# The start of a hybrid decoder step: weights by contraction tiles in a written order, and one unit of the decode's logits moved behind the projections

## The chip, the cores and the metric

The kernel runs on one core of one Trainium2 chip. A core has five engines that run side by side and wait for one another through semaphores: TensorE (PE, matrix products and transposes, with its own stream of weight loads, PEld), VectorE (DVE), ScalarE (ACT), GpSimd (POOL) and SyncE (SP), which here only issues transfers. SP, POOL and ACT put transfers on queues that sixteen DMA engines serve. Products are accumulated in PSUM, in banks of 512 float32 columns. The metric is the device time of one execution in microseconds; before the change it is 1644.03 us, the median of three runs (1642.79 to 1644.74).

## The reference

One layer of a decoder step for 512 prompt rows, 16 learned meta rows ahead of them and 8 x 4 sample rows that continue sequences with 512 cached positions. All 560 rows are normalized and multiplied by one combined weight of 2048 x 12288; what comes out is used by a stick-breaking attention and a gated short convolution; both are merged, projected and normalized once more. Everything is float32.

```python
h = rmsnorm(x, g_pre)
q, k, v, ga, cb, cc, ch, gc, ma, mc = split(h @ w_in)
a = stick_breaking(q, k, v) * silu(ga)            # prompt: its own rows; samples: cached pages, then own rows
c = cb * causal_conv3(cc * ch) * silu(gc)
m = sigmoid(ma + b_ga) * (a @ w_pa) + sigmoid(mc + b_gc) * (c @ w_pc)
y = x + rmsnorm(m @ w_out, g_post)

# stick_breaking for one head
z = q @ k.T * d ** -0.5 + b_sb                     # logits
log_keep = where(s < t, log_sigmoid(-z), 0)
after = reverse_cumsum(log_keep) - log_keep
out = where(s < t, exp(log_sigmoid(z) + after), 0) @ v
```

## The kernel before

Rows of activations lie transposed: `h_hi` and `h_lo` hold the normalized rows as 16 contraction tiles of 128 by 560 rows. A float32 product is made of three products of a reduced type: each operand is split in a high part (a cast on ACT) and the rest (a subtraction on DVE), and a product is high by high, high by low, low by high. So each weight tile of 128 x 1024 costs a load on SP's queue, a cast `whi` on ACT, a subtraction `wlo` on DVE and 24 products for each range of rows. Five raw buffers (`wraw`) and three pairs of split buffers (`whl`) go round.

**The start** (lines 143 to 363) normalizes the 560 rows in five tiles, 0 to 4, and makes the first four query heads (`FIRST`). `norm_stats` loads a tile, squares and sums its rows on ACT and takes Ln and Exp for a first reciprocal root, which `newton` mends with five small operations of one column on DVE. `norm_half` multiplies half a tile by that root and the gain (DVE), transposes eight blocks on PE into two PSUM tiles, copies them as high parts (ACT), and returns the function that later subtracts the low parts (DVE). The PSUM tiles for the transposes come round from three banks `z` and one `t`. The gain is spread over the partitions by 32 small products and four copies on DVE (`g_copy`). `q_load` brings the weights of one query head in two tiles, one for each half of the contraction, in rows of 128 columns; `q_part` multiplies all 16 contraction tiles for one head. The rows come in two ranges (`START`), the first of 256 rows, which the token tiles 0 and 1 fill. What is wrapped in `pin` (`keep_in_program_order`) keeps the written order on its engine; the rest is ordered by a planner that simulates a timeline and prefers earlier program order, or whatever stands in `high_priority`. Here DVE's work is pinned, while loads, ACT's work and PE's products and transposes are left to the planner, the transposes with high priority.

**Projections** (824 to 833): for heads 0 to 3 `head_now` makes keys, values and another query head and attends at once; for heads 4 to 7 `head_later` makes keys and values only. **Pairs** (1016 to 1042): 4 pairs of the attention's gate, 16 of the convolution, 16 of the merge gates, each two columns of weights by seven products instead of eight (`seven`, line 887). **w_pc stage** (1079 to 1095): the convolution's output by `w_pc`, the last four heads' attention, and the decode's values. Then `w_pa`, merge, `w_out` and the output norm.

**The decode** (`decode_steps`, a generator) is spread over these stages. Its logits are 16 units of four pages each, a page being one step: two products and sums over 128 x 1024 elements on DVE and ACT (lines 689 to 700), with loads on POOL's queue. `DEC1` units belong to the part `"part"`, which the projections call up: five steps in each `head_now`, four in each `head_later`, until the part is used up. The others belong to `"logits"` and are called up by `dec_group` behind each of the 36 pair groups: groups 1 to 4 take 2, 1, 2, 1 steps, groups 5 to 20 one each, 21 to 31 two and one in turn from two on, group 32 all that is left. Then come two softplus pieces, the weights (two exponentials) and the values: 64 pages of 256 KB through seven buffers `vpage`, multiplied on PE at line 784. The first value pages have to be asked for by the end of the pairs (line 1043).

Of the kernel before, what the change touches and what calls it, by code (L numbers as in the profile page):

```python
# [9 lines left out]
F32 = mybir.dt.float32  # L10
# [7 lines left out]
P = 128  # L18
# [29 lines left out]
DEC1 = 6  # L48
# [12 lines left out]
def hybrid_step_kernel(  # L61
# [64 lines left out]
    def rstd_of(eng, out, ss, tmp, n, w=1, later=False):  # L126

        v, r, t = (tmp[:n, i * w:(i + 1) * w] for i in range(3))
        act.activation(r, ss, AF.Ln, bias=eps_c[:n], scale=1.0 / D)
        act.activation(r, r, AF.Exp, scale=-0.5)  # L130
# [54 lines left out]
    def norm_stats(i):  # L185

        n = sum(r[0] for r in XT[i][0])
        xt = sp.tile([P, D], F32, name="xt", bufs=3)[:n]
        load_x(xt, i)
        ss = sp.tile([P, 1], F32, name="ss", bufs=5)[:n]  # L190
# [3 lines left out]
        with tc.high_priority():  # L194
            act.activation(sq, xt, AF.Square, accum_out=ss)
            newton = rstd_of(dve, rs, ss, tmp, n, later=True)
        return (i, n, xt, rs), newton

    def norm_half(c, x):
# [7 lines left out]
        low = []  # L207
        for kq in range(2):
            pt = next(start_ps)()
            pv = pt[:, :4 * n].rearrange("p (k t) -> p k t", t=n)  # L210
            with tc.high_priority(2000):
                for k in range(4):
                    pe.transpose(out=pv[:, k, :], in_=hn[:, (4 * kq + k) * P:(4 * kq + k + 1) * P],
                                 identity=ident[:n, :n])
            k0 = 8 * c + 4 * kq
            for r0, r1, t0 in XT[i][1]:
                dst = (slice(None), slice(k0, k0 + 4), slice(t0, t0 + r1 - r0))
                with tc.high_priority(2000):
                    act.copy(h_hi[dst], pv[:, :, r0:r1])
                low.append((h_lo[dst], pv[:, :, r0:r1], h_hi.bitcast(F32)[dst]))  # L220

        def lows():
            for x in low:
                pin(dve.tensor_sub(*x))
        return lows


    def w_load(src, pl=wraw):
        raw = pl.tile([P, 8, P], F32, tag="raw", name="raw", bufs=5 if pl is wraw else 2 * FIRST - 5)
# [53 lines left out]
    w_low = []  # L283

    def low(n=1):

        for _ in range(n):
            unit, raw = w_low.pop(0)
            lo = whl.tile([P, 8, P], F32R, tag="lo", name="wlo")
# [1032 lines left out]
```

## Time and profile before

| what | us |
|---|---|
| median of three runs (lowest, highest) | 1644.03 (1642.79, 1644.74) |
| the profiled execution's own time | 1641.85 |
| its span, first to last instruction | 1640.3 |
| busy in the span: PE / DVE / ACT / POOL | 1594.9 / 1251.8 / 970.1 / 232.4 |
| start, until the first product of the projections | 86.4 |
| projections | 86 to 386 |
| pairs | 386 to about 1176 |
| w_pc stage | about 1176 to 1342 |

The times in the timeline rows are microseconds from the span's first instruction: start, length, engine, line, operation, what is written and read, its size. In brackets stands how long the engine had been idle and what ended that. Lengths of products overlap, since the next starts while one drains; what a product costs is the distance to the next start. An engine's name with a q (SPq) is its issuing of transfers.

### The profile page before, as it was taken

What the parts mean: (1) busy time and instruction counts of PE and PEld (TensorE: products, weight loads), DVE (VectorE), ACT (ScalarE), POOL (GpSimd) and SP (SyncE); (2) the same over time, 40 slices, a digit from 0 to 9 for tenths busy, and PEclk for the clock granted to TensorE, in tenths of its full rate; (3) what the DMA queues carried; (4) which work ended last, traced back from release to release, by engine and by line L of the source; (5) the groups of instructions that cost most, each with busy time, mean ns of one, the idle gap of its engine ahead of it and who ended that gap; (6) DMA issues with size and microseconds to landing.
All of it is one profiled execution on the core that took longest, in us unless ns stands there. A gap on an engine that the chain in (4) does not pass through costs nothing.

```text
span 1640.3 us, 31584 instructions
## 1 busy us (share of the span) xinstructions
PE 1594.9 (97%) x12176; PEld 1531.3 (93%) x12176; DVE 1251.8 (76%) x1707; ACT 970.1 (59%) x2529; POOL 232.4 (14%) x414
## 2 busy tenths in 40 slices
PE   7999999999999999999999999999999999999996
PEld 6999999999999999999999999989867699999995
DVE  4537887797988988888988888876555567877774
ACT  5237887745765655655677667685544543455552
POOL 0033233322101010101011010013122110000000
PEclk7999999999999999999999999999999999999998
DMA  9255454445544444443455454446887555433336
GB/s 228 70 179 152 155 160 139 146 128 170 157 147 136 136 135 122 127 142 111 137 164 161 149 174 148 135 125 204 283 261 222 172 152 179 154 106 94 104 87 216
DMA packets 306492, 252.72 MB, mean 154 GB/s; under 512 B 11457, under 2 KB 276741, under 8 KB 305237
## 3 DMA queue, kind: packets, MB, share of 16 engines
q1 hardware_dynamic: 277605, 159.73, 34.1%
q0 software_dynamic: 28016, 88.80, 16.5%
q8 instruction: 95, 1.56, 0.4%
q10 hardware_dynamic: 720, 2.17, 0.4%
q14 instruction: 56, 0.46, 0.1%
HBM read 217.95 MB, written 32.71 MB: 153 GB/s over the span
## 4 chain that ended last, share of the span: by engine, by line
PE 75%; ACT 6%; DMA 5%; DVE 5%; issue 3%; POOL 0%; DVEq 0%; SPq 0%; POOLq 0%; ACTq 0%
PE mm L887 24%; PE mm L252 24%; PE o L887 19%; ACT junk L695 3%; PE tp L784 2%; ACT whi L236 2%; DMA raw<-in_w_in 2%; PE z L614 1%; PE o L624 1%; DVE pr L689 1%; DVE wlo L237 1%; DMA gt<-gate_scr 1%; PE z L545 1%; PE z L887 1%; DMA kpage<-in_cache_k 1%
## 5 line engine op out<-in xcount | busy, mean ns | idle before, releaser
L236 ACT CAST whi<-raw 128x1024 fp32r<-128x1024 f32 x251 | 263.1, 1050 | 258.5 <-PE o L887 79.3
L237 DVE TENSOR_TENSOR wlo<-raw,whi 128x1024 fp32r<-128x1024 f32 x251 | 306.4, 1221 | 58.0 <-ACT whi L236 46.1
L887 PE MATMUL mm<-h_hi,whi 128*128 128x272 f32 (+1 forms) x1152 | 333.5, 290 | 2.8 <-ACT whi L236 2.8
L887 PE MATMUL mm<-h_lo,whi 128*128 128x272 f32 (+1 forms) x1152 | 332.1, 288 | 0.0
L887 PE MATMUL mm<-h_hi,wlo 128*128 128x272 f32 (+1 forms) x1152 | 331.3, 290 | 0.0
L887 PE MATMUL o<-t_hi,whi 128*128 128x272 f32 (+1 forms) x864 | 252.2, 292 | 8.5 <-ACT o L901 5.9
L887 PE MATMUL o<-t_hi,wlo 128*128 128x272 f32 (+1 forms) x864 | 249.9, 289 | 1.4 <-DVE wlo L237 1.4
L887 PE MATMUL o<-t_lo,whi 128*128 128x272 f32 (+1 forms) x864 | 249.6, 289 | 0.0
L237 DVE TENSOR_TENSOR wlo<-s,whi 128x1024 fp32r<-128x1024 f32 x126 | 154.2, 1224 | 101.5 <-ACT whi L236 101.2
L887 PEld LDWEIGHTS mm<-h_hi,whi 128*128 128x128 f32 x1152 | 217.3, 189 | 5.5 <-ACT whi L236 3.7
L887 PEld LDWEIGHTS mm<-h_hi,wlo 128*128 128x128 f32 x1152 | 216.3, 189 | 0.6 <-DVE dr L412 0.4
L887 PEld LDWEIGHTS mm<-h_lo,whi 128*128 128x128 f32 x1152 | 216.8, 188 | 0.1
L695 ACT ACTIVATE junk<-pr 128x128 f32<-128x128 f32 x592 | 182.7, 309 | 28.3 <-DVE pr L689 16.1
L236 ACT CAST whi<-s 128x1024 fp32r<-128x1024 f32 x126 | 131.6, 1044 | 97.5 <-PE o L887 31.0
L252 PE MATMUL mm<-h_hi,whi 128*128 128x280 f32 (+1 forms) x640 | 187.1, 293 | 0.0
L252 PE MATMUL mm<-h_hi,wlo 128*128 128x280 f32 (+1 forms) x640 | 187.0, 293 | 0.0
L252 PE MATMUL mm<-h_lo,whi 128*128 128x280 f32 (+1 forms) x640 | 186.7, 292 | 0.0
L887 PEld LDWEIGHTS o<-t_hi,whi 128*128 128x128 f32 x864 | 162.7, 188 | 15.1 <-ACT o L901 7.0
L887 PEld LDWEIGHTS o<-t_hi,wlo 128*128 128x128 f32 x864 | 162.9, 189 | 2.3 <-DVE wlo L237 2.2
L887 PEld LDWEIGHTS o<-t_lo,whi 128*128 128x128 f32 x864 | 163.4, 189 | 0.0
L689 DVE TENSOR_TENSOR pr<-kpage,qb 128x1024 f32<-128x1024 f32 x128 | 152.3, 1218 | 8.4 <-DMA kpage<-in_cache_k 4.0
L252 PEld LDWEIGHTS mm<-h_hi,whi 128*128 128x128 f32 x640 | 120.5, 188 | 0.7
(389 smaller groups left out, 3398.2 us busy)
## 6 DMA issues: line engine op xcount, KB each, us to landing
raw<-in_w_in SPq DMA_DIRECT2D x192, 512.0 KB, 4.3
kpage<-in_cache_k POOLq DMA_DIRECT2D x64, 256.0 KB, 3.4
qb<-q_scr POOLq DMA_DIRECT2D x32, 512.0 KB, 5.3
vpage<-in_cache_v POOLq DMA_DIRECT2D x64, 256.0 KB, 5.7
raw<-in_w_out SPq DMA_DIRECT2D x32, 512.0 KB, 4.0
gate_scr<-g POOLq DMA_DIRECT2D x32, 272.0 KB, 3.2
gt<-gate_scr POOLq DMA_DIRECT2D x16, 544.0 KB, 4.2
raw<-in_w_pc SPq DMA_DIRECT2D x16, 512.0 KB, 5.8
```

What stands on the lines that cost most here:

```text
L236: act.copy(hi, x)
L237: dve.tensor_sub(lo, x, hi.bitcast(F32))
L252: pe.matmul(o, lhsT=w, rhs=r[:, t0:t1], start=(k == 0 and n == 0), stop=(k == nk - 1 and n == 2))
L545: pe.matmul(zt[:m, c0:c0 + n], lhsT=l[:, s0:s0 + m], rhs=r[:, ts:ts + n], start=(c0 == 0 and i == 0), stop=(i == 2), skip_group_check=True)
L614: pe.matmul(o, lhsT=l, rhs=x, start=False, stop=(i == len(ops) - 1), skip_group_check=True)
L624: pe.matmul(ot[:, ts - NMETA:ts - NMETA + n], lhsT=l[:m, st, :], rhs=x[:m, c0:c0 + n], start=False, stop=(g == GROUPS[-1] and i == 2), ski ...
L689: dve.tensor_mul(pr, kt.unsqueeze(1).broadcast_to([P, 2, 512]), qt))
L695: act.activation(junk, pr[:, t, h * P:(h + 1) * P], AF.Copy, accum_out=z_all[:, pg, b, 4 * hf + h, 2 * i + t:2 * i + t + 1])
L784: pe.matmul(po[32 * j:32 * (j + 1), :], lhsT=lhs, rhs=rhs, start=(pg == 0), stop=(pg == NPG), tile_position=(0, 32 * j), skip_group_check= ...
L887: pe.matmul(o, lhsT=l[:, k, :], rhs=r, start=(start and k == 0 and m == 0), stop=(stop and k == 7 and m == 2), skip_group_check=True)
```

## The change

The start is written out as one order for every engine: loads of token tiles, statistics, transposes, high parts and products are pinned too. The query weights come as eight tiles of two contraction tiles by four heads, in rows of 512 columns; `q_chunk` multiplies two contraction tiles for all four heads as soon as these are there, over the first range of rows. Two of the gain's copies go to ACT, the Newton operations of tiles 2 and 4 to POOL, the bank `o` joins the transposes' round, and the four accumulators of the first range share two banks. Tile 2 comes before tile 4, and tile 3 last. `DEC1` becomes 5, and the groups take 2 steps each up to the fourth, one each up to 20, two and one in turn up to 33, where the logits end.

```diff
-DEC1 = 6
+DEC1 = 5
...
-            nc.sync.dma_start(xt[r:r + n, :], {"p": xp, "m": meta_tokens, "s": xs}[src][r0:r0 + n, :])
+            tc.keep_in_program_order(
+                nc.sync.dma_start(xt[r:r + n, :], {"p": xp, "m": meta_tokens, "s": xs}[src][r0:r0 + n, :]))
...
     def g_copy(c):
-        pin(dve.tensor_copy(g_bc[:, c * 512:(c + 1) * 512], g_ps[c]))
+        copy = dve.tensor_copy if c < 2 else act.copy
+        pin(copy(g_bc[:, c * 512:(c + 1) * 512], g_ps[c]))
-    start_ps = cycle((z_ps, z_ps, z_ps, t_ps))
+    start_ps = cycle((z_ps, z_ps, z_ps, t_ps, o_ps))
...
-        with tc.high_priority():
-            act.activation(sq, xt, AF.Square, accum_out=ss)
-            newton = rstd_of(dve, rs, ss, tmp, n, later=True)
-        return (i, n, xt, rs), newton
+        pin(act.activation(sq, xt, AF.Square, accum_out=ss))
+        return (i, n, xt, rs), rstd_of(eng, rs, ss, tmp, n, later=True, fix=pin)
...
-            with tc.high_priority(2000):
-                for k in range(4):
-                    pe.transpose(out=pv[:, k, :], in_=hn[:, (4 * kq + k) * P:(4 * kq + k + 1) * P],
-                                 identity=ident[:n, :n])
+            for k in range(4):
+                pin(pe.transpose(out=pv[:, k, :], in_=hn[:, (4 * kq + k) * P:(4 * kq + k + 1) * P],
+                                 identity=ident[:n, :n]))
...
+        def highs():
+            for dst, src in parts:
+                pin(act.copy(h_hi[dst], src))
...
+    def by_k(tile_):
+        return tile_.rearrange("p (k h) c -> p k h c", k=2)
+    def q_load():
+        c = len(q_raw)
+        raw = wraw.tile([P, 8, P], F32, tag="raw", name="raw")
+        pin(nc.sync.dma_start(raw.rearrange("p (k h) c -> p k (h c)", k=2),
+                              win[2 * c * P:2 * (c + 1) * P, GATE_Q:GATE_Q + FIRST * P].rearrange(
+                                  "(k p) c -> p k c", p=P)))
+        q_raw.append(raw)
+    def q_part_tile(c, name):
+        if c < 3:
+            return whl.tile([P, 8, P], F32R, tag=name, name="w" + name)
+        return sp.tile([P, 8, P], F32R, name="w" + name, bufs=NC - 3)
+    def q_high():
+        c = len(q_hi)
+        q_hi.append(q_part_tile(c, "hi"))
+        pin(act.copy(q_hi[c], q_raw[c]))
+    def q_low():
+        c = len(q_lo)
+        q_lo.append(q_part_tile(c, "lo"))
+        pin(dve.tensor_sub(q_lo[c], q_raw[c], q_hi[c].bitcast(F32)))
+    def q_product(o, h, k, n, start, stop):
+        t0, t1 = START[n]
+        hi, lo = (by_k(x[k // 2])[:, k % 2, h, :] for x in (q_hi, q_lo))
+        for m, (l, r) in enumerate(((hi, h_hi), (hi, h_lo), (lo, h_hi))):
+            pin(pe.matmul(o, lhsT=l, rhs=r[:, k, t0:t1], start=(start and m == 0), stop=(stop and m == 2),
+                          skip_group_check=True))
+    def q_chunk(c):
+        for h in range(FIRST):
+            for k in (2 * c, 2 * c + 1):
+                q_product(q_o[h], h, k, 0, k == 0 and h % 2 == 0, k == KD - 1)
+    def keep_warm(n):
+        pass
...
+    X[0], X[1] = x_load(0), x_load(1)
+    for _ in range(3):
+        q_load()
+    X[2] = x_load(2)
+    X[0], newton0 = norm_stats(X[0])
+    g_copy(0), g_copy(1)
+    g_copy(2), g_copy(3)
+    X[1], newton1 = norm_stats(X[1])
+    newton0(pin)
+    h00, l00 = norm_half(0, X[0])
+    h01, l01 = norm_half(1, X[0])
+    h00()
+    newton1(pin)
+    q_high()
+    h10, l10 = norm_half(0, X[1])
+    h01()
+    l00()
+    h11, l11 = norm_half(1, X[1])
+    h10()
+    X[4] = x_load(4)
+    for _ in range(2):
+        q_load()
...
+    l10()
+    q_high()
+    q_low()
+    h11()
+    q_chunk(0)
+    l01()
+    q_low()
+    l11()
+    q_high()
+    q_chunk(1)
+    X[2], newton2 = norm_stats(X[2], pool)
+    q_low()
+    for _ in range(2):
+        q_load()
+    q_chunk(2)
+    X[4], newton4 = norm_stats(X[4], pool)
+    newton2()
+    h20, l20 = norm_half(0, X[2])
+    q_high()
+    q_low()
+    q_load()
+    X[3] = x_load(3)
+    h20()
+    q_chunk(3)
+    h21, l21 = norm_half(1, X[2])
+    q_high()
+    l20()
+    q_low()
+    h21()
+    newton4()
+    q_chunk(4)
+    h40, l40 = norm_half(0, X[4])
+    l21()
+    q_high()
+    h40()
+    q_low()
+    h41, l41 = norm_half(1, X[4])
+    q_chunk(5)
+    l40()
+    h41()
+    q_high()
+    q_low()
+    l41()
+    q_chunk(6)
+    q_high()
+    q_low()
+    X[3], newton3 = norm_stats(X[3])
+    q_chunk(7)
+    newton3(pin)
+    h30, l30 = norm_half(0, X[3])
+    h30()
+    h31, l31 = norm_half(1, X[3])
+    h31()
+    l30()
+    l31()
...
+    for h in range(FIRST):
         q_o[h] = (z_ps if h < 3 else mm_ps)()[:, :START[1][1] - START[1][0]]
-        q_part(q_o[h], q_w[h], 1, (0, 1, 2), True, True)
-        low(min(len(w_low), 2))
+        for k in range(KD):
+            q_product(q_o[h], h, k, 1, k == 0, k == KD - 1)
...
-        if n <= 31:
-            dec_step(1 if 4 < n <= 20 else 1 + n % 2, "logits")
-        elif n == 32:
-            dec_step(64, "logits")
-            dec_step(1)
+        if n <= 33:
+            dec_step(1 if 4 < n <= 20 else 2 if n <= 4 else 1 + n % 2, "logits")
+            if n == 33:
+                dec_step(64, "logits")
         else:
             dec_step(1)
```

More of the change, by code (lines that the diff above doesn't have):

```diff
@@ L189, in norm_stats @@
         load_x(xt, i)
+        return i, n, xt
+    def norm_stats(x, eng=dve):
+        i, n, xt = x
         ss = sp.tile([P, 1], F32, name="ss", bufs=5)[:n]
@@ L206, in norm_half @@
                                      op0=ALU.mult, op1=ALU.mult))
-        low = []
+        parts = []
         for kq in range(2):
@@ L210, in norm_half, with w_load @@
             pv = pt[:, :4 * n].rearrange("p (k t) -> p k t", t=n)
-            with tc.high_priority(2000):
-                for k in range(4):
-                    pe.transpose(out=pv[:, k, :], in_=hn[:, (4 * kq + k) * P:(4 * kq + k + 1) * P],
-                                 identity=ident[:n, :n])
+            for k in range(4):
+                pin(pe.transpose(out=pv[:, k, :], in_=hn[:, (4 * kq + k) * P:(4 * kq + k + 1) * P],
+                                 identity=ident[:n, :n]))
             k0 = 8 * c + 4 * kq
             for r0, r1, t0 in XT[i][1]:
[L217 to L220, printed above, removed]
+                parts.append(((slice(None), slice(k0, k0 + 4), slice(t0, t0 + r1 - r0)), pv[:, :, r0:r1]))
+        def highs():
+            for dst, src in parts:
+                pin(act.copy(h_hi[dst], src))
         def lows():
[L223 to L229, printed above, removed]
+            for dst, src in parts:
+                pin(dve.tensor_sub(h_lo[dst], src, h_hi.bitcast(F32)[dst]))
+        return highs, lows
+    def w_load(src):
+        raw = wraw.tile([P, 8, P], F32, tag="raw", name="raw")
         nc.sync.dma_start(raw, src.rearrange("(k p) c -> p k c", p=P))
@@ L282, in hybrid_step_kernel @@
     START = ((HM, HM + 256), (HM + 256, T))
[L283 to L289, printed above, removed]
-            pin(dve.tensor_sub(lo, raw, unit[0].bitcast(F32)))
-            unit.append(lo)
-    def q_part(o, ws, n, parts, start, stop):
-        t0, t1 = START[n]
-        for k in range(KD):
-            for m in parts:
-                pe.matmul(o, lhsT=ws[k // 8][m // 2][:, k % 8, :], rhs=(h_lo if m == 1 else h_hi)[:, k, t0:t1], start=(start and k + m == 0),
-                          stop=(stop and k == KD - 1 and m == parts[-1]), skip_group_check=True)
@@ L300, in hybrid_step_kernel @@
-    q_w, q_o = [], []
-    def q_load(h):
-        q_w.append([])
-        for src in win_srcs(GATE_Q + h * P):
-            n = len(w_low)
-            raw = w_load(src, sp if n >= 5 else wraw)
-            hi = sp.tile([P, 8, P], F32R, name="whi", bufs=2 * FIRST - 3) if n >= 3 else \
-                whl.tile([P, 8, P], F32R, tag="hi", name="whi")
-            act.copy(hi, raw)
-            q_w[h].append([hi])
-            w_low.append((q_w[h][-1], raw))
-    x0, newton0 = norm_stats(0)
-    x1, newton1 = norm_stats(1)
@@ L345, in hybrid_step_kernel @@
-    l21 = norm_half(1, x2)
-    l20()
-    newton3(pin)
-    l30 = norm_half(0, x3)
-    l21()
-    l31 = norm_half(1, x3)
-    l30()
-    low()
-    l31()
-    low()
-    for h in range(FIRST):
-        q_part(q_o[h], q_w[h], 0, (2,), False, True)
+    q_high()
[9 more added lines that the diff above has]
+    q_high()
```

41 lines of the change are left out of this document (14 added, 27 removed).

## The prediction

> **What bounds the kernel now.** I read the page's busy table first, then the busy time in windows, stage by stage. The columns of a window row are: length, then busy time and instructions of TensorE, its weight loads, VectorE (DVE), ScalarE (ACT) and, where it ran, GpSimd (POOL), then granted clock, DMA share, GB/s.
>
> ```profile
> span 1640.3 us, 31584 instructions
> PE 1594.9 (97%) x12176; PEld 1531.3 (93%) x12176; DVE 1251.8 (76%) x1707; ACT 970.1 (59%) x2529; POOL 232.4 (14%) x414
> ...
> 0.00:26.39 26.39, 14.47 (x67) 11.76 (x67) 12.66 (x31) 15.64 (x24) 2.15 (x9) 0.67 1.02 245
> 26.39:53.44 27.05, 24.32 (x192) 23.35 (x192) 17.71 (x41) 13.63 (x29) 0.00 (x0) 0.94 0.45 107
> 53.44:86.40 32.96, 32.96 (x249) 32.96 (x249) 12.99 (x13) 5.72 (x9) 2.21 (x4) 1.00 0.35 100
> ...
> 86.00:386.00 300.00, 298.87 (x2296) 291.39 (x2294) 231.53 (x322) 208.53 (x672) 94.07 (x164) 1.00 0.48 148
> 490.00:833.00 343.00, 341.64 (x2697) 340.48 (x2696) 305.29 (x369) 205.49 (x545) 27.41 (x48) 1.00 0.44 130
> 833.00:1054.00 221.00, 216.29 (x1698) 214.22 (x1698) 185.47 (x179) 153.85 (x448) 23.95 (x42) 1.00 0.52 155
> 1160.00:1360.00 200.00, 198.88 (x1319) 157.95 (x1318) 121.45 (x261) 97.72 (x164) 35.28 (x65) 1.00 0.68 216
> ```
>
> TensorE is the bound from 53 us to the end of these windows. Of the first 26.39 us it is busy 14.5, at a granted clock of 0.67. So time saved in the start moves everything behind it forward one for one; time taken from DVE or ACT in a stage where TensorE has no gap is worth nothing, and time put there costs only the gaps it opens. The timeline of TensorE shows what the start is made of:
>
> ```profile
> 8.62 1.33 PE L175 MATMUL z<-g_hl,pick 16*128 16x128 f32 x8
> ...
> 13.78 0.42 PE L213 MATMUL z<-ident,hn 128*128 128x128 f32 x1
> 13.99 0.42 PE L213 MATMUL tp<-ident,hn 128*128 128x128 f32 x1
> ...
> 22.07 1.97 PE L213 MATMUL z<-ident,hn 128*128 128x128 f32 x8 [6.80 <-DVE h_lo L224]
> 26.39 1.01 PE L297 MATMUL mm<-h_hi,whi 128*128 128x256 f32 x3 [2.35 <-ACT h_hi L219]
> ...
> 38.97 0.28 PE L297 MATMUL mm<-h_lo,whi 128*128 128x256 f32 x1
> ...
> 42.18 0.28 PE L297 MATMUL o<-h_hi,whi 128*128 128x256 f32 x1
> 44.93 1.06 PE L213 MATMUL z<-ident,hn 128*128 128x128 f32 x8 [2.48 <-DVE hn L205]
> ...
> 47.02 0.27 PE L213 MATMUL tp<-ident,hn 128*128 128x128 f32 x1
> 47.13 0.27 PE L213 MATMUL z<-ident,hn 128*128 128x128 f32 x1
> ...
> 83.81 0.30 PE L297 MATMUL mm<-h_hi,wlo 128*128 128x296 f32 x1
> ...
> 86.27 0.30 PE L297 MATMUL mm<-h_hi,wlo 128*128 128x296 f32 x1
> 86.40 0.29 PE L252 MATMUL mm<-h_hi,whi 128*128 128x280 f32 x1
> ```
>
> From one start to the next, a product with 256 columns takes 0.119 us (27 intervals from 38.97 to 42.18), one with 296 takes 0.137 (18 from 83.81 to 86.27), a transpose 0.21 on the slow clock and 0.11 on the full one. The four first query heads are 192 products of each width: 22.8 + 26.2 = 49.0 us. They start at 26.39 and the next projection starts at 86.40, so 11.0 us of those 60 are transposes, slow clock (the middle window: 27.05 us at 0.94, so 3.2 us at half rate, 1.6 lost) and waits.
>
> **The change, the start.** Products, transposes, normalizations and splits stay the same in number. The weights now come as eight tiles of two contraction tiles by four heads, so the first products need only an eighth of the weights and the first half of two token tiles. The order is written out, so I walked it down, each engine in order, with these durations (ACT, then DVE):
>
> ```profile
> 10.28 1.91 ACT L195 ACTIVATE sq<-xt 128x2048 f32<-128x2048 f32 x1 [1.71 <-DMA xt<-in_x_prompt]
> ...
> 31.12 0.58 ACT L219 CAST h_hi<-z 128x512 fp32r<-128x512 f32 x1
> 31.60 0.59 ACT L219 CAST h_hi<-tp 128x512 fp32r<-128x512 f32 x1
> 36.68 1.92 ACT L195 ACTIVATE sq<-xt 128x2048 f32<-128x2048 f32 x1 [4.49 <-DMA xt<-in_x_prompt]
> ...
> 39.16 1.90 ACT L195 ACTIVATE sq<-xt 128x2048 f32<-128x2048 f32 x1
> ...
> 47.75 0.14 DVE L133 TENSOR_SCALAR rtmp<-ss 128x1 f32<-128x1 f32 x1
> ...
> 48.58 1.28 DVE L205 SCALAR_TENSOR_TENSOR hn<-xt,rs,g_bc 128x1024 f32<-128x1024 f32 x1
> 49.78 0.68 DVE L224 TENSOR_TENSOR h_lo<-z,h_hi 128x512 fp32r<-128x512 f32 x1
> 50.38 0.68 DVE L224 TENSOR_TENSOR h_lo<-tp,h_hi 128x512 fp32r<-128x512 f32 x1
> ...
> 56.23 2.35 DVE L290 TENSOR_TENSOR wlo<-raw,whi 128x1024 fp32r<-128x1024 f32 x2
> ```
>
> So a tile's statistics occupy ACT for 2.5 us (36.68 to 39.16), a copy of 512 columns 0.48; the five Newton operations take DVE 0.83, a normalized half 1.2, a low part 0.6, a weight's low part 1.15. A weight's cast on ACT I take at 0.95, twice the copy of half its width.
>
> ACT: the second tile lands at 10.28. The two gain copies that move from DVE to ACT end by 10.5 (the last gain product starts 8.62 and runs 1.33), so they cost the chain 0.2. Statistics end 13.0, two copies 14.0, first weight cast 14.9, next copies 15.9, and those of the second tile 17.9, behind their transposes. DVE: Newton 13.1 to 13.9, half 15.2, low parts 16.4, half 17.6, low parts 18.8, first weight's low part 19.9, and the next low part at 20.6 frees the PSUM bank that the last four transposes of the second tile want (three banks go round). Those run to 21.6, and behind them in TensorE's queue stands the first chunk of 24 products. It starts at 21.6 instead of 26.39. The clock is slow then: 3.2 us at half rate as now, so the chunk ends at 25.7, the next two at 28.6 and 31.4.
>
> From there a chunk takes 24 x 0.119 = 2.85 us and half a tile's eight transposes 0.88; for the fifth tile, of 48 tokens, I estimate half of that. Chunk 3 ends 35.1, chunk 4 38.8. The fifth tile's second normalized half is written ahead of chunk 5 and comes from DVE at 40.3, so TensorE waits 1.0; it waits 0.5 more for a low part before chunk 6. Chunk 7 ends at 50.0, the last tile's transposes at 51.8, its first low parts at 52.7, and 26.2 us of wide products end at 79.0. With 0.1 us more at each handover the same walk ends at 79.4, with 0.15 at 80.1. I take 79.6: a **gain of 6.8 us** against 86.40, bounds 6.1 (ending at 80.3) and 7.5. Afterwards the next projection can't be late: the three weight slots that it needs are the first chunks', last read by head 3 at 73 to 75, and cast plus low part take 2.2.
>
> Loads: the first 26.39 us move 245 GB/s. A tile of 128x2048 is 1.05 MB, a weight 0.52. The walk wants the third token tile (4.7 MB into the queue) by 23.3 and the fourth weight (5.6 MB) by 28.3; 4.7 MB take 19.2 us at that rate, 5.6 take 22.9. On SP's queue the fifth tile waits for the first one's buffer, free at 12, with two weights behind it; the sixth weight waits for the first low part at 20, and the last tile stands behind the eighth weight, issued at 25 and wanted at 44. Weight rows grow from 512 B to 2 KB, which I count as nothing.
>
> Two Newton chains move to GpSimd, whose own arithmetic this trace shows only in other shapes:
>
> ```profile
> 0.43 0.10 POOL L1310 MEMSET const-float32-0.0<- 128x1 f32 x1 [0.43 <-issue]
> ...
> 1127.08 0.94 POOL L716 TENSOR_SCALAR_AFFINE_SELECT z_new<-z_new 32x256 f32<-32x256 f32 x1
> ```
>
> Between 0.10 and 0.94 an operation I take 0.35, nearer to the memset, which has the same single column. The chain then runs 25.9 to 27.7, the half it feeds ends at 29.0, and TensorE wants it at 31.4: up to 0.85 us an operation is free, and at 1.0 the walk ends at 80.3. [...]
>
> **The change, the decode.** The loop over heads asks for 20 page steps in the first four heads and 16 in the last four; 6 units of 4 pages are 24 steps, 5 are 20. So the four steps of head 4 leave a stage where TensorE waits 1.1 us in 300: gain 0. They go to the second and fourth group of pairs, which get two steps instead of one, and to groups 32 and 33; the softplus, weights and value loads behind them come a group or two later.
>
> ```profile
> 425.00:446.00 21.00, 21.00 (x169) 21.00 (x168) 18.23 (x20) 13.47 (x37) 2.37 (x4) 1.00 0.47 143
> 446.00:468.00 22.00, 22.00 (x177) 22.00 (x177) 19.98 (x22) 17.07 (x57) 2.90 (x5) 1.00 0.60 189
> ...
> 1121.92 4.08 POOL L667 DMA_DIRECT2D vpage<-in_cache_v  x7
> ...
> 1160.00:1200.00 40.00, 40.00 (x291) 34.44 (x290) 24.00 (x42) 25.34 (x41) 4.47 (x9) 1.00 0.95 302
> 1200.00:1240.00 40.00, 38.90 (x239) 27.73 (x238) 24.39 (x54) 18.00 (x33) 10.55 (x21) 1.00 0.70 223
> ...
> vpage<-in_cache_v POOLq DMA_DIRECT2D x22, 256.0 KB, 5.7
> ```
>
> Among the gating pairs the group with two steps (446 to 468) leaves TensorE without a gap: 0 for the two early ones. The gate window 833 to 1054 has five groups with two steps and 4.7 us of gaps, 0.9 a group at most; conv's sixteen with one step have 1.4 in all. So a gate group with a second step costs up to 0.9; with 0.3 for the early ones I take **1.2**, bounds 0 and 3.
>
> The value pages begin at 1121.92, two groups before the pairs end, and 22 of 64 are issued by 1160: 5.8 MB. Two groups later they meet the conv rows, w_pc weights and gate rows of the next stage, where 40 us already run at 0.95 DMA share and 302 GB/s. TensorE's work there is only moved. What can be lost is a wait behind pages in the queue: at least 0, at most the seven pages that the buffers hold, 1.84 MB or 6.1 us at 302 GB/s. TensorE waits just 1.1 us in that stage now, at that load, so I take a quarter, **1.6**.
>
> Sum: -6.8 + 1.2 + 1.6 = -4.0. The profiled execution, 1641.85 us (1640.3 of span and 1.55 around it), becomes 1637.9; the median of the runs shown is 1644.03, 2.2 above it, and becomes **1640.0**.
>
> **The rivals.**
> - *The boundary costs nothing* and the start all it can: -7.5 to -6.8, plus 0.3: 1636.8 to 1637.5, say 1637.2. For it: TensorE's 198.9 of 200 us; against it: 0.95 DMA share.
> - *Handovers eat the walk*: tightly pinned queues let one late engine hold three others, and half of the gain goes: -3.4 + 2.8: 1643.4. For it: in the old start the waits of 6.8, 2.35 and 2.48 us are of this kind; against: from the first chunk on, the walk has TensorE wait at three places and leaves less than 1 us to spare at only one more.
> [...]
> - *Slower: value pages against conv rows.* All 22 pages displace transfers that TensorE waits for, not seven: 5.8 MB at 302 GB/s are 19.2 us. Half of it exposed is +9.6: -6.8 + 1.2 + 9.6 = +4.0, 1648.0. It decides from 8.9 us of exposed waiting in 1160 to 1240. For it: 0.95 share; against: the pages wait on their own seven buffers, so they can't all be ahead.
> - *The written order is what the planner already had*: then only the costs stay, +2.8, 1646.8. Against it: the chunks need a weight layout that doesn't exist before.
>
> **How the numbers follow.** What a measurement of this kernel can tell from no change is about 0.2%, 3.3 us: faster is below 1640.7, slower above 1647.3. Forecast 0.43 (its own range 1638.3 to 1641.7, three quarters of it below 1640.7), boundary free 0.15, handovers 0.15, GpSimd 0.12, pages 0.12 (nearly all above 1647.3), no new order 0.03 (half above). Faster 0.32 + 0.15 = 0.47; slower 0.13; same 0.40. The range 1636 to 1648 leaves out the deep ends of the boundary and pages cases, some 0.1 together.
>
> **What would show it.** The first products at 21 to 23 us, the last wide one at 79 to 80.5, and the next projection right behind it. TensorE's gap before the fifth tile's second half about 1 us. [...] No visible gap in 425 to 490 moved forward by 7; the first value page near the last gate group, not two ahead. Waits of TensorE for gt, c_hl or whi of w_pc in the 80 us behind the pairs above 5 us in sum would mean the pages case; a product start later than 25 us, or a last wide product after 83, would make the sum wrong at its first term.

## The result

The changed kernel takes 1653.55 us, the median of 11 runs (1649.38 to 1657.24), beside 1643.79 (1641.24 to 1647.73) for the kernel before on the same chip. The ratio is 1.0061, with a 95% interval from 1.0052 to 1.0070: some 10 us **slower**, where 1640.0 was forecast and the range ended at 1648. The profiled execution took 1653.55 us itself. Its page begins:

```profile
span 1651.9 us, 31577 instructions
PE 1605.4 (97%) x12176; PEld 1538.7 (93%) x12176; DVE 1246.8 (75%) x1695; ACT 963.9 (58%) x2540; POOL 235.6 (14%) x424
```

The work is the same 12176 matmuls, and they are counted as busy 10.5 us longer. To see where, I cut both traces at the same products: the end of the start, of the projections, of the first convolution pair, the middle of the second pair, the end of the convolution, two gate groups later, the twelfth of the 16 gate groups, and the last product. Windows of the kernel before (columns as in the prediction):

```profile
86.40:379.30 292.90, 291.77 (x2239) 284.33 (x2238) 226.89 (x318) 204.30 (x665) 92.52 (x162) 1.00 0.49 149
379.30:553.80 174.50, 171.56 (x1354) 170.62 (x1353) 149.51 (x171) 109.90 (x293) 22.32 (x38) 1.00 0.51 154
553.80:596.50 42.70, 42.70 (x338) 42.70 (x337) 35.67 (x43) 25.31 (x67) 1.64 (x3) 1.00 0.42 122
...
811.30:856.40 45.10, 42.92 (x338) 42.44 (x337) 38.61 (x38) 34.67 (x107) 5.25 (x9) 1.00 0.53 161
...
1073.10:1624.50 551.40, 545.01 (x4041) 497.23 (x4039) 373.26 (x634) 280.04 (x552) 66.38 (x119) 1.00 0.55 170
```

And of the changed kernel:

```profile
19.60:75.40 55.80, 55.03 (x435) 54.58 (x434) 29.31 (x43) 23.15 (x42) 8.10 (x14) 0.98 0.43 133
75.40:373.60 298.20, 293.08 (x2238) 285.82 (x2237) 210.81 (x305) 192.05 (x601) 87.92 (x158) 0.99 0.47 140
373.60:551.60 178.00, 173.91 (x1354) 172.27 (x1353) 155.07 (x177) 117.03 (x333) 23.36 (x40) 0.99 0.52 153
551.60:599.40 47.80, 44.48 (x338) 44.26 (x337) 35.59 (x43) 25.38 (x67) 3.12 (x5) 0.96 0.46 131
...
815.90:863.90 48.00, 44.74 (x338) 44.05 (x337) 38.52 (x38) 34.55 (x107) 5.30 (x9) 0.96 0.54 151
...
1081.40:1636.10 554.70, 549.33 (x4040) 498.89 (x4039) 380.81 (x640) 277.94 (x585) 65.84 (x119) 1.00 0.55 169
```

Read the lengths in pairs. The start ends 11.0 us earlier (75.4 against 86.4): more than the 6.8 forecast. Then every stage takes some back: the projections 5.3 (298.2 against 292.9), the gating pairs and the first convolution pair 3.5, half a convolution pair 5.1 (47.8 against 42.7), the rest of the convolution 1.7, the first two gate groups 2.9, ten more 0.8, and everything behind them 3.3. Sum 22.6, so the last product is 11.7 us later. A stage's length less TensorE's busy time is what TensorE waits there: from the end of the start to the last product 26.9 us, against 16.4 in the kernel before. So 10.5 of the 22.6 us are waits. The clock column shows a second part: TensorE's granted clock is 1.00 in all of these stages before, and 0.96 in two of the short ones now.

TensorE's waits in the changed kernel, worst first (in total, times, longest):

```profile
PE o L949 <- DVE c L975: 8.9, 8, 3.3
PE tp L505 <- DVE ks L511: 4.0, 1, 4.0
...
PE mm L256 <- DVE gt L1156: 3.1, 1, 3.1
```

The row of the kernel before that answers to the first of them:

```profile
PE o L887 <- DVE c L913: 2.6, 4, 1.5
```

**The projections.** The timeline of the changed kernel around the first page step of head 0:

```profile
105.75 0.50 POOL L541 DMA_DIRECT2D q_scr<-qn  x1 [3.50 <-ACT nat L506]
108.52 2.17 POOL L744 DMA_DIRECT2D qb<-q_scr  x3 [2.26 <-issue]
...
114.29 1.22 DVE L752 TENSOR_TENSOR pr<-kpage,qb 128x1024 f32<-128x1024 f32 x1 [8.33 <-DMA qb<-q_scr]
...
115.96 0.66 PE L505 MATMUL tp<-ident,raw 128*128 128x128 f32 x4 [4.02 <-DVE ks L511]
```

and the kernel before:

```profile
115.78 1.23 DVE L689 TENSOR_TENSOR pr<-kpage,qb 128x1024 f32<-128x1024 f32 x1 [3.15 <-DMA qb<-q_scr]
```

The decode's query rows go to memory (`q_scr`) and come back spread over the partitions (`qb`). They land at 114.3 instead of 115.8: this chain moved forward by 1.5 us while TensorE moved forward by 11. VectorE stands in front of the first page product for 8.33 us, its copies `nat` and `ks` are queued behind it, and TensorE waits 4.02 us for `ks`.

**The second convolution pair.** Timeline of the changed kernel:

```profile
554.65 0.74 POOL L744 DMA_DIRECT2D qb<-q_scr  x1 [1.16 <-DVE pr L752]
...
555.94 0.71 POOL L744 DMA_DIRECT2D qb<-q_scr  x1
567.47 1.23 DVE L961 TENSOR_TENSOR s<-raw 128x1024 f32<-128x1024 f32 x1 [3.82 <-DMA raw<-in_w_in]
...
569.75 2.35 DVE L752 TENSOR_TENSOR pr<-kpage,qb 128x1024 f32<-128x1024 f32 x2
...
573.16 0.44 DVE L975 TENSOR_TENSOR c<-o,s 128x274 f32<-128x274 f32 x1
573.65 0.40 PE L949 MATMUL o<-t_hi,whi 128*128 128x274 f32 x1 [3.32 <-DVE c L975]
```

In the kernel before, these loads are issued in the middle of a pair, and at this place the sums have their weights in time (over all pairs they wait for weights 14 times in both kernels, 14.0 us in sum and 2.6 at most before, 17.3 and 3.8 now):

```profile
514.41 0.76 POOL L681 DMA_DIRECT2D qb<-q_scr  x1 [0.88 <-DVE pr L689]
...
519.28 0.73 POOL L681 DMA_DIRECT2D qb<-q_scr  x1
...
565.87 1.22 DVE L899 TENSOR_TENSOR s<-raw 128x1024 f32<-128x1024 f32 x1
```

A unit of four page steps begins with the loads of two query tiles and a page. With 2 steps in each of the first four groups (8 steps) a unit begins with a convolution pair, each of which has four groups; with 2, 1, 2, 1 (6 steps) it begins in the middle. In the changed kernel the weights are 3.82 us late for the sums on VectorE, two page products (2.35 us) stand between the sums and `c` as they did before, and TensorE waits 3.32 us for `c`. That the query loads are what holds the weights up is read from the order of the loads; no run took them away here.

**Five waits are paid a second time.** Windows of the changed kernel just behind three of them:

```profile
404.00:408.00 4.00, 4.00 (x22) 4.00 (x21) 4.00 (x5) 2.56 (x10) 0.00 (x0) 0.59 0.15 54
...
575.00:579.00 4.00, 4.00 (x23) 4.00 (x23) 3.47 (x4) 1.06 (x6) 0.00 (x0) 0.63 0.00 0
...
1186.00:1190.00 4.00, 4.00 (x18) 3.18 (x16) 3.88 (x7) 0.00 (x0) 2.15 (x4) 0.63 0.96 303
```

Four microseconds without a gap, 18 to 23 matmuls, at a granted clock of 0.6. There are five such stretches between 90 us and the last product, each 3.4 us long at half rate (behind 116, 404, 574, 837 and 1185 us); at 1.7 us each they are 8.5 us. The kernel before has none in that range. With the 10.5 us of waits this is 19.0 of the 22.6; of the other 3.6, 2.6 lie behind the gates (see e8).

**The boundary.** In the changed kernel the value pages start 46 us later than in the kernel before (1121.92), and run into the next stage's rows. VectorE stands 7.32 us for the rows `sg`, `gt` is queued behind them, and TensorE waits for `gt`:

```profile
1168.18 4.06 POOL L730 DMA_DIRECT2D vpage<-in_cache_v  x7
...
1184.21 0.69 DVE L1127 TENSOR_TENSOR sg<-sg 128x512 f32<-128x512 f32 x1 [7.32 <-DMA sg<-a_scr]
...
1185.46 0.78 PE L256 MATMUL mm<-c_hl,whi 128*128 128x272 f32 x2 [3.15 <-DVE gt L1156]
```

### The profile page after: what moved, and what is told of

Read it like the earlier page. It is cut to its first block, busy times and chain, and to the rows that moved or that the text cites. A ratio compares the mean times of both kernels' runs of the same rounds, so it can differ in the third digit from the quotient of the medians.

```text
span 1651.9 us, 31577 instructions
## 1 busy us (share of the span) xinstructions
PE 1605.4 (97%) x12176; PEld 1538.7 (93%) x12176; DVE 1246.8 (75%) x1695; ACT 963.9 (58%) x2540; POOL 235.6 (14%) x424
## 4 chain that ended last, share of the span: by engine, by line
PE 76%; DVE 5%; ACT 5%; DMA 5%; issue 3%; DVEq 0%; POOL 0%; SPq 0%; POOLq 0%; ACTq 0%
PE mm L256 25%; PE mm L949 23%; PE o L949 19%; PE tp L847 3%; ACT junk L758 2%; DMA raw<-in_w_in 2%; ACT whi L240 2%; DVE pr L752 2%; PE z L677 1%; PE o L687 1%; DVE wlo L241 1%; PE z L608 1%; PE z L949 1%; DMA sg<-a_scr 1%; DMA kpage<-in_cache_k 1%
## 5 line engine op out<-in xcount | busy, mean ns | idle before, releaser
L752 DVE TENSOR_TENSOR pr<-kpage,qb 128x1024 f32<-128x1024 f32 x128 | 151.5, 1216 | 13.9 <-DMA qb<-q_scr 13.2
```

Of the source, the lines that this page charges most:

```text
L752: dve.tensor_mul(pr, kt.unsqueeze(1).broadcast_to([P, 2, 512]), qt))
```

## Experiments

All were timed in five rounds against the kernel before. The table gives the ratio with its interval, that ratio in us of about 1642, and from each profile how far the same product of TensorE lies behind (+) or ahead (-) of the kernel before, in us, at the cuts named above. "late" means that head 0's first page step is written behind the values' projection.

| kernel | ratio (95%) | us | start's end | proj. end | conv pair 1 | pair 2 mid | conv end | gate 2 | gate 12 | last |
|---|---|---|---|---|---|---|---|---|---|---|
| changed | 1.0061 (1.0052-1.0070) | +10.0 | -11.0 | -5.7 | -2.2 | +2.9 | +4.6 | +7.5 | +8.3 | +11.7 |
| e1 start alone, 6 units | 1.0031 (1.0019-1.0042) | +5.1 | -10.6 | -4.8 | +3.1 | +3.3 | +3.4 | +3.6 | +3.5 | +3.5 |
| e2 decode's part alone | 1.0066 (1.0044-1.0087) | +10.8 | +0.2 | +0.7 | +4.5 | +6.2 | +10.8 | +11.6 | +12.5 | +17.2 |
| e3 changed, first rows from x | 1.0048 (1.0031-1.0065) | +7.9 | -8.1 | -5.5 | -3.7 | -0.8 | +2.8 | +4.1 | +5.2 | +9.9 |
| e4 = e1 + late | 0.9975 (0.9964-0.9985) | -4.1 | -11.2 | -7.9 | -4.6 | -4.6 | -4.6 | -4.4 | -4.4 | -3.4 |
| e5 = changed + late | 1.0046 (1.0033-1.0059) | +7.6 | -8.1 | -3.8 | -0.6 | +3.3 | +6.2 | +5.4 | +7.3 | +10.4 |
| e6 = changed, groups 2,1,2,1 | 1.0038 (1.0024-1.0053) | +6.2 | -10.5 | -4.7 | -4.1 | -4.1 | -4.1 | -3.0 | -1.7 | +6.2 |
| e7 = before, groups 2,2,2,2 | 1.0007 (0.9999-1.0016) | +1.1 | -0.7 | -0.3 | +1.6 | +5.9 | +8.1 | +8.0 | +8.0 | +5.8 |
| e8 = e6 + late | 1.0014 (1.0003-1.0026) | +2.3 | -11.2 | -7.6 | -7.3 | -7.3 | -7.4 | -4.9 | -3.6 | +3.3 |
| e9 = e8, steps spread | 1.0038 (1.0024-1.0051) | +6.2 | -8.1 | -4.3 | -3.9 | -3.9 | -3.9 | +0.2 | +9.3 | +13.0 |
| e10 = e4, groups 1,2,1,2 | 0.9963 (0.9951-0.9976) | -6.1 | -11.1 | -6.1 | -4.8 | -4.8 | -4.8 | -4.5 | -3.6 | -3.3 |
| e11 = changed, 4 buffers qn | 1.0068 (1.0055-1.0081) | +11.2 | -8.1 | -1.5 | +0.9 | +5.9 | +10.2 | +10.8 | +11.2 | +14.8 |
| e12 = e10, 4 buffers qn | 0.9984 (0.9973-0.9995) | -2.6 | -11.9 | -6.1 | -4.6 | -4.6 | -4.6 | -2.8 | -2.3 | -2.4 |

One profile is one execution. Those of e2, e5, e7, e9, e10 and e11 are the slowest of their runs, 1.5 to 5.4 us above the median, so a row is read for places and the ratio for size. In e3, e5, e9 and e11 the start itself ran 3 us later (see the last section), so their columns up to the projections' end don't compare with the others.

**e1, the start alone.** The changed kernel with

```diff
-DEC1 = 5
+DEC1 = 6
...
-        if n <= 33:
-            dec_step(1 if 4 < n <= 20 else 2 if n <= 4 else 1 + n % 2, "logits")
-            if n == 33:
-                dec_step(64, "logits")
+        if n <= 31:
+            dec_step(1 if 4 < n <= 20 else 1 + n % 2, "logits")
+        elif n == 32:
+            dec_step(64, "logits")
+            dec_step(1)
```

> The new start with 6 units beside the projections and the groups' old steps. Theory A (the start gains 11 us, gives some 5 back at the first page step of the decode's logits, and the rest of the loss belongs to the moved unit): projections end about 5.7 us earlier than before, nothing is lost in the pairs or at the boundary to the w_pc stage, time about 5.7 below the kernel before (1638 where that has 1643.8). Theory B (the written start spoils the planner's order of what follows, and the moved unit is harmless): time as the changed kernel, 9 to 10 above the kernel before.

Neither: +5.1 us. The start's 10.6 us are there, 5.8 go in the projections and 7.9 by the end of the first convolution pair, and next to nothing behind. Of the 7.9, 3.8 are waits (6.7 against 2.9) and 3.4 are two half-rate stretches. Windows and the longest wait:

```profile
380.00:385.00 5.00, 4.26 (x21) 4.04 (x21) 3.85 (x4) 2.00 (x2) 2.64 (x5) 0.66 0.66 189
...
400.00:404.00 4.00, 2.90 (x14) 2.90 (x15) 4.00 (x6) 1.91 (x5) 0.00 (x0) 0.68 0.45 134
```

```profile
401.10 0.39 PE L950 MATMUL o<-t_hi,whi 128*128 128x272 f32 x1 [3.21 <-DVE c L976]
```

So a shorter start alone makes this kernel slower; its gain is gone without the moved unit.

**e2, the decode's part alone.** The kernel before with the opposite edit: `DEC1 = 5` and the new `dec_group`.

> The old start with 5 units beside the projections and the groups' new steps. Theory A: start and projections as before, some 3 us lost in the first four pair groups, some 10 more until group 32 (weights that land late behind the query rows of a new unit, and the slow clock after the wait), and some more behind the pairs; 12 to 17 us above the kernel before. Theory B: within 3 us of the kernel before.

+10.8 us (7 to 14), as much as the whole change and a little less than theory A's 12 to 17. Its profile, the slowest of six runs, lies 17.2 behind: 4.5 by the first convolution pair's end, 6.3 in the convolution behind it, 1.7 in the gates and 4.7 behind them.

**e3, the first query rows without their detour.** The changed kernel, but the first unit multiplies by rows of the sample's input instead of the queries, so its logits are left out.

```diff
-                        pool.dma_start(qt, q_scr[r0:r0 + 2, cs].unsqueeze(0).broadcast_to([P, 2, 512]))
+                        pool.dma_start(qt, (xs if hf + b == 0 else q_scr)[r0:r0 + 2, cs].unsqueeze(0).broadcast_to([P, 2, 512]))
```

> The changed kernel, but the first unit of the decode's logits multiplies its pages by rows of x_sample instead of the queries, which leaves the queries of one sequence's first four heads out of the result; its row loads then wait for no projection. Theory A (VectorE stands 8.3 us at the first page's product because the query rows, which come out of the four first heads through a scratch, land only then, and TensorE waits 4.0 us for a copy queued behind it): that wait of TensorE is gone, and the half clock behind it too, some 5 us below the changed kernel. Rival (VectorE would be late there anyway): same time as the changed kernel.

2.1 us less than the changed kernel by the ratios, less than half of theory A's 5. TensorE's wait of 4.0 and the half-rate stretch behind it are gone, but it still waits 3.4 us in the projections (5.1 in the changed kernel), most of it for the copies `qn`, whose buffer waits for its store. The projections lose 2.6 instead of 5.3, but start 3 us later, and end at the same place (-5.5 and -5.7). So the rows' way through memory is a part of that loss, not all of it, and this profile can't tell how large a part.

**e4, the first step later.** e1 with

```diff
-        dec_step(1, "part")
+        dec_step(int(h > 0), "part")
         vhi, vlo = v_proj(h, np_)
-        dec_step(1, "part")
+        dec_step(1 + int(h == 0), "part")
```

> The new start with 6 units and the old steps of the groups, and the first page step of the decode written behind head 0's value projection instead of ahead of it. Theory A: the query rows have landed by then, the wait of 4 us is gone: 4 to 6 us below the start alone, about 1633. Rival (the wait only moves to the next thing that stands behind the page's product): as the start alone, within 2 us.

1638.08 us, 9.2 us under e1 by the ratios and **faster than both kernels**. The trace divides this: the projections lose 3.3 instead of 5.8, and the stretch up to the first convolution pair's end 3.3 instead of 7.9. In the projections the rival is right about the waits: TensorE waits 4.5 us in sum where it waited 4.4, now for other copies (`qn`, `nat`, `hi`) and at most 1.7 us at a time. What is gone is the slow stretch behind the long wait: in e1, behind a wait of 2.93 us ahead of 115.64, a product of 272 columns starts every 0.23 us; behind e4's wait of 1.15 ahead of 117.99 it is every 0.13, and e4's projections are 2.5 us shorter. Why the second part eases so far from the edit (waits of 3.3 instead of 6.7 us, one half-rate stretch instead of two) isn't resolved; all steps there are the same.

**e5, the changed kernel with that edit.**

> The changed kernel (5 units beside the projections, the new early groups) with the first page step of head 0 written behind the values' projection instead of in front of it. Theory E (the start's gain is lost at this step, whatever follows): the gap of 4.0 us at 116 and the half-rate stretch behind it go, the projections end 2 to 4 us earlier than in the changed kernel (373.5), and the time is 5 to 8 us lower, about 1646 to 1648. Rival: the step was late because the query rows land late in the changed kernel; the wait moves one step down, the projections end at 373 as before, and the time stays at 1652 to 1654.

+7.6, 2.4 us under the changed kernel, less than half of what theory E wanted. The large wait at 116 and the half-rate stretch are gone, but as in e4 shorter waits stand in its place: 5.2 us in the projections, against 5.1 in the changed kernel. They end at 375.5 instead of 373.6, in a profile whose start ran 3 us later. The convolution behind its first pair costs 6.8 us in both kernels (-0.6 to +6.2).

**e6 and e7, the place of the units in the pairs.** e6 is the changed kernel, e7 the kernel before, with the first four groups exchanged:

```diff
-            dec_step(1 if 4 < n <= 20 else 2 if n <= 4 else 1 + n % 2, "logits")
+            dec_step(1 if 4 < n <= 20 else 1 + n % 2, "logits")
```

(e7 has it the other way round.)

> The changed kernel, but the first four groups of the pairs take 2, 1, 2, 1 steps as before the change instead of 2 each; the two steps that are left over run with group 33. Units of four page steps then begin in the middle of each convolution pair, as before the change, instead of at its first step. Theory F (the place of the unit's first step in the pair is what costs): the waits at 573 and 836 for the convolution's sums go, 5 to 8 us of the convolution's and the gates' loss come back, two more steps at group 33 cost about 2, the time is about 1647 to 1650. Rival G (each step added to the pairs has its price wherever it stands): the loss moves to group 33 and the time stays between 1651 and 1656.

> The kernel before the change (6 units beside the projections, old start) with 2 steps in each of the first four groups. No work is moved out of the projections; only the place of the units in the pairs changes, and the last logits come one group earlier. Theory F: the convolution loses 5 to 8 us as in the changed kernel, the time is 1648 to 1652 on the scale on which the kernel before has 1643.8. Rival G: no work was added, the time is 1642 to 1645.

e6 came out at the upper end of theory F, 3.8 us under the changed kernel, although its two left-over steps cost more behind the gates (7.9 us from gate group 12 to the end, against 3.4). e7 came out as rival G says, +1.1. The traces decide for the place. Between the first convolution pair's end and the middle of the second, the six kernels with 2, 2, 2, 2 steps (changed, e2, e3, e5, e7, e11) lose 1.7 to 5.1 us; the seven others lose nothing (0 to 0.2). Only the price is less than F had it, and e7 earns 2.2 us at the end, where its logits are done a group earlier.

**e8 and e9, both remedies.** e8 is e6 with e4's edit; e9 moves e8's two left-over steps from group 33 into gate groups 22 and 24:

```diff
-            dec_step(1 if 4 < n <= 20 else 1 + n % 2, "logits")
+            dec_step(2 if n in (22, 24) else 1 if 4 < n <= 20 else 1 + n % 2, "logits")
```

> The changed kernel (5 units beside the projections) with both remedies: the first page step of head 0 behind the values' projection, and 2, 1, 2, 1 steps in the first four groups, so that the two steps left over run with group 33. Theory H (the moved unit itself is cheap; the two unlucky places and the burst behind group 33 cost): without the two places only the burst is left, some 4 us, and the time lies 4 to 6 us above that of the start alone with the first step later (1638.1): 1642 to 1644. Rival G (a unit moved to the pairs has its price wherever it stands, about 10 us as in the run of the decode's part alone): 1647 to 1650.

> As the run before in this list, but the two steps left over run one each with the gate groups 22 and 24 instead of with group 33, so that no burst stands in front of the last products. Theory H: 2 to 4 us below that run, 1639 to 1641, since a gate group with two steps was seen to wait nowhere in the kernel before. Rival G: the same time as that run, 1646 to 1650.

e8 is at +2.3, between the two and nearer to H. Beside e4 (-4.1) the moved unit costs 6.4 us even with both places mended, and the windows from gate group 12 to the last product say where: e4,

```profile
1068.70:1621.10 552.40, 546.45 (x4041) 498.65 (x4039) 373.24 (x634) 280.04 (x552) 66.21 (x119) 1.00 0.55 170
```

and e8:

```profile
1069.40:1627.80 558.40, 549.67 (x4041) 499.27 (x4039) 386.74 (x646) 291.86 (x629) 66.36 (x120) 1.00 0.55 168
```

6.0 us longer, at the same number of matmuls: 2.8 of it are idle time, 3.2 lie inside matmuls that are counted as busy. Most of the 3.2 is found at the 128 products of value pages. Idle time taken off, they take 37.9 us to the next start instead of 35.9: a product of another kind follows one of them 36 times instead of 33, and starts 0.52 us later, where the next value product starts 0.2 us later. In the changed kernel they take 39.8 (38 times), in the kernel before 35.7 (33 times).

For e9, H fails and the time is G's: the end costs less (3.7), but the gates lose 13.2 us (-3.9 to +9.3). The two steps shift the units against the gate groups, and the timeline of e9 shows the same wait as in the convolution:

```profile
851.47 0.59 PE L949 MATMUL o<-t_hi,whi 128*128 128x272 f32 x1 [3.30 <-DVE c L975]
```

**e10, the second part's first steps apart.** e4 with 1, 2, 1, 2 steps in the first four groups:

```diff
-            dec_step(1 if 4 < n <= 20 else 1 + n % 2, "logits")
+            dec_step(1 if 4 < n <= 20 else 2 - n % 2 if n <= 4 else 1 + n % 2, "logits")
```

> The start alone with the first page step later (6 units; 1638.1) and 1, 2, 1, 2 steps in the first four groups instead of 2, 1, 2, 1: the first page of the second part is followed by no second step in its group. Theory J (the wait of 0.9 us at 403 and the half-rate stretch behind it come from two page steps queued in one group while the first query rows land): both go, 2 to 3 us less, about 1635 to 1636. Rival: the rows land late in any case, 1637.5 to 1639.

1636.12 us, as theory J has it, and the best kernel of the study, though its interval overlaps e4's. The half-rate stretch that e4 has here,

```profile
404.00:408.00 4.00, 4.00 (x23) 4.00 (x23) 3.24 (x4) 3.07 (x17) 0.00 (x0) 0.63 0.21 73
```

is gone in e10:

```profile
404.00:408.00 4.00, 4.00 (x34) 4.00 (x33) 3.33 (x3) 1.89 (x4) 0.00 (x0) 1.00 0.30 88
```

But its profile, the slowest of five runs, has another one at 120, behind a wait of 2.5 us for `nat`, and ends no further ahead than e4's (-3.3 and -3.4); the gain of 2 us rests on the runs' times alone.

**e11 and e12, four buffers for the query rows.** The changed kernel and e10 with

```diff
-        qn = hp.tile([TS, P], F32, name="qn", bufs=1)
+        qn = hp.tile([TS, P], F32, name="qn", bufs=4)
```

> The changed kernel with four buffers instead of one for the sample's query rows (qn) on their way to the scratch in memory. Theory K (behind the shortened start the projections run into the chain copy, store, next copy of these rows: the copies at 96.05, 100.57 and 103.47 each stand 1.2 to 3.6 us for the store before them, so the query rows land at 114.3, only 1.5 us earlier than in the kernel before, and the first page step with the copies behind it is late): with four buffers the waits of the copies go, the last store is issued at about 100 instead of 105.75, the rows land at about 109, TensorE's waits of 1.1 at 101 and 4.0 at 116 and the half-rate stretch go, the projections end about 4 to 5 us earlier, near 369, and the time is 3 to 5 us lower than the changed kernel's 1653.6. Rival: the rows are held by the queue's own time from issue to landing, the wait stays near 4 us and the time within 1.5 us.

> The start alone with the first page step of head 0 later and 1, 2, 1, 2 steps in the first four groups (1636.1), with four buffers for the query rows. Theory K: TensorE's wait of about 1.1 us at 101 goes and what the projections lost against their start (75.3 to 373.2) shrinks by 1 to 3 us: 1633 to 1635.5. Rival: nothing is left to gain there since the first step is already behind the values' projection, 1635.5 to 1637.

Theory K falls: +11.2 and -2.6, no gain; e12 is even 3.5 us above e10. ScalarE's copies no longer stand, but the stores on GpSimd's queue come no sooner (the last one at 108.65 instead of 105.75, in a profile whose start ran 3 us later; in e12 at 105.23, in e10 at 105.57), and the loads come later: 114.36 instead of 108.52, in e12 110.27 and in e10 108.20. The timeline of e11:

```profile
108.65 0.50 POOL L541 DMA_DIRECT2D q_scr<-qn  x1 [3.50 <-issue]
114.36 2.18 POOL L744 DMA_DIRECT2D qb<-q_scr  x3 [5.21 <-issue]
...
118.52 1.23 DVE L752 TENSOR_TENSOR pr<-kpage,qb 128x1024 f32<-128x1024 f32 x1 [10.89 <-DMA qb<-q_scr]
...
120.18 1.12 PE L505 MATMUL tp<-ident,raw 128*128 128x128 f32 x4 [6.58 <-DVE ks L511]
```

What keeps the stores 3.5 to 4.2 us apart on that queue, and the loads 5.7 us behind the last store, stays open.

## Why the prediction was wrong

From e4 to the changed kernel the ratios give a path in three edits: e4 -4.1; with the unit moved (e8) +2.3; with the new early groups (e5) +7.6; with head 0's first step early (the changed kernel) +10.0. So 6.4, 5.3 and 2.4 us, each uncertain by 2.5 to 3, so the last one isn't clear of zero. The parts don't simply add up: the later step is worth 9.2 us from e1 to e4, 3.9 from e6 to e8 and 2.4 here. The trace of the changed kernel sums to -11.0 + 5.3 + 14.0 + 3.4 = +11.7, where the forecast had -6.8 + 0 + 1.2 + 1.6. None of its bounds let the projections or the pairs lose more than 3 us, so the range could not hold the time.

- **The start, -6.8.** Right in its mechanism and too small: 11.0. The timeline of the changed kernel has the points that the walk named:

```profile
18.84 1.11 PE L216 MATMUL z<-ident,hn 128*128 128x128 f32 x4 [0.43 <-DVE h_lo L228]
19.61 0.56 PE L321 MATMUL mm<-h_hi,whi 128*128 128x256 f32 x1
...
38.05 0.42 PE L216 MATMUL o<-ident,hn 48*128 48x48 f32 x4 [0.77 <-DVE hn L209]
...
75.26 0.30 PE L321 MATMUL mm<-h_hi,wlo 128*128 128x296 f32 x1
```

  The first chunk starts at 19.6 (21.6 forecast), because the last four transposes waited only 0.43 us for a bank: the one that they got was freed by an earlier low part than the walk assumed. The first range ends at 48.9 (52.8 in the walk), and the clock is at 0.98 from 19.6 to 75.4. The wait ahead of the fifth tile's second half is 0.77 us (1.0), the last wide product starts at 75.3 (79.6).
- **"Time saved in the start moves everything behind it forward one for one."** This is the step that failed. It looked at TensorE alone. The next stage also hangs on a chain outside TensorE, the query rows' way through memory, and this had 3.15 us of waiting on VectorE already in the kernel before, where no wait of TensorE stood behind it. The long start hid it. The chain moved forward by 1.5 us, TensorE by 11.0, and the projections gave back 5.3: TensorE's waits there grew from 1.1 to 5.1 us, and a half-rate stretch added 1.7. e1 shows it without the moved unit: 5.8 of 10.6 us go in the projections, and the rest and more up to the first convolution pair's end. e4, with that step later, is 4.1 us faster than the kernel before, but TensorE waits as long in its projections as in e1's; only the waits are shorter, and no half-rate stretch follows there. So the gain doesn't come through whole even with the first page out of the way, and what holds up the copies for which TensorE then waits stays open (e3, e11).
- **Head 4's steps, 0.** The windows had said that TensorE waits 1.1 us in 300; right that nothing was to be gained there (e2's projections take 293.4 us, against 292.9).
- **The pairs, +1.2 (bounds 0 to 3).** Mis-sized by far: 14.0 us from the projections' end to gate group 12 in the trace of the changed kernel (3.5 + 5.1 + 1.7 + 2.9 + 0.8). I priced a group with two steps by its gaps and didn't ask what the two early steps move: the start of every later unit, with its two query loads, from the middle of a convolution pair to its beginning. e6 against the changed kernel shows it, 3.8 us by the ratios. Counting gaps also leaves out the slow stretches: the waits of 1.89, 3.32 and 2.08 us here (ahead of 403.54, 573.65 and 836.56) were each followed by 3.4 us at a granted clock of 0.50, 5.1 of the 14.0 us.
- **The boundary, +1.6 (bounds 0 to 6.1).** Inside its bounds, at twice the value: 3.1 to 4.7 us from gate group 12 to the end in the six kernels with 5 units and the new or the spread groups, 6.9 and 7.9 in e8 and e6, where the burst of left-over steps runs with group 33. The mechanism was only partly the one that was priced, so that the value fell inside is partly luck. The wait for `gt` (3.15 us, at most 1.1 before) is the kind that the pages rival named, below its 8.9 us. But TensorE's waits in this stretch are 5.4 us in sum, against 6.4 in the kernel before. The loss is the half-rate stretch behind that wait (1.7) and 2.6 us in products counted as busy, the value pages' above all.
- **GpSimd's chain** (0.35 us an operation in the walk, and a chance of 0.12 for a late one) was not late. The timeline of the changed kernel:

```profile
25.54 0.19 POOL L138 TENSOR_TENSOR rs<-rtmp 128x1 f32<-128x1 f32 x1
...
27.44 1.25 POOL L136 TENSOR_TENSOR rtmp<-rtmp 48x1 f32<-48x1 f32 x1
...
27.42 1.22 DVE L315 TENSOR_TENSOR wlo<-raw,whi 128x1024 fp32r<-128x1024 f32 x1 [0.37 <-ACT whi L310]
```

  Of the ten operations in the two chains, the six that began while VectorE stood took 0.19 to 0.20 us, the four that began beside one of its operations (`wlo` or `hn`) 1.10 to 1.25. The first chain ends at 25.7 (forecast 27.7), in good time for the half that it feeds.

## What to carry to other kernels

Before a saved microsecond is moved forward through the next stages, look there for every wait of another engine that has no TensorE wait behind it yet: it is the next bound, and here the next stage took back about half. A step that is moved shifts the start of all later units of its loop against the stage they run beside; price its first instruction (its loads, and what stands behind them), not its average. Try the parts of a change apart: one part here was worth 4 to 6 us and the other cost more than that.

## What was not expected of the hardware

Waits of up to 4 us were followed by 3.4 us at half the granted clock, but not always. In the changed kernel this happened behind waits of 1.89 to 4.02 us; in the kernel before a wait of 3.15 us that ended at 1082.41 was not followed by it:

```profile
1082.40:1086.40 4.00, 3.99 (x31) 3.99 (x32) 2.12 (x4) 3.99 (x6) 0.00 (x0) 1.00 0.37 106
```

In the traces of these two kernels all changes of the granted clock lie whole multiples of 3.413 us apart (from 117.17 to 403.88 us, 84 of them, in the changed kernel), and each of the five slow stretches is one such step at 0.50. I cut both traces from 60 us to the last product into these steps. In the changed kernel half clock followed the five steps at full clock in which TensorE stood 1.89, 2.08, 2.21, 2.51 and 3.15 us in sum; the next lower sum, 1.81 us in the step from 110.34, was not followed by it. In the kernel before the highest sums are 1.75 and 1.40 us, the two parts into which a step's end cut the wait before 1082.41, and no step was followed by half clock. No limit can be read from this: in e12 a wait of 1.77 us ahead of 849.20 was followed by products 0.23 us apart, against 0.13 before it. The wait before 1082.41 had no price; that of 1.89 us ahead of 403.54 lay in one step and cost 1.7 us more. So which waits are paid twice is partly a matter of where they fall, and the number of slow stretches in a profile is partly luck. No run here tried the clock by itself.

The same start took 3 us longer in four of the profiles (e3, e5, e9, e11), in which the 24 products that spread the gain took 5.4 us instead of 3.0. The timeline of the changed kernel, where the first products follow at 19.61:

```profile
5.31 3.01 PE L176 MATMUL mm<-g_hl,pick 16*128 16x128 f32 x24
```

and of e5, where they follow at 22.57:

```profile
5.90 5.38 PE L176 MATMUL mm<-g_hl,pick 16*128 16x128 f32 x24
```

The ten GpSimd operations of one column, for which the forecast had one figure, 0.35 us, took 0.9 to 1.1 us longer beside a VectorE operation than without one (0.19 to 0.20 and 1.10 to 1.25 us, in the changed kernel's trace): in the rows above 1.25 us instead of 0.19, beside a VectorE operation of 1.22.
